# Differential attention in a written order of steps, and the last FFN tile's last accumulator in two passes of 256 columns

## The chip, the core and the metric

The kernel runs on one core of a Trainium2 chip. The core has five engines that each work through their own queue of instructions: PE (TensorE, matrix products into the accumulator memory PSUM), DVE (VectorE), ACT (ScalarE), POOL (GpSimd) and SP (SyncE, which here only issues DMA transfers). They meet through semaphores. Loading a matmul's stationary operand is shown as a row of its own (PEld). PSUM has eight banks of 128 × 512 float32.

The metric is device time in microseconds of one execution of the whole program. Lower is better.

## What is computed

A two-layer decoder trunk on 512 tokens with 1024 features. Layer 0 mixes latent attention and differential attention, layer 1 dilated and stick-breaking attention; each is followed by a gated ConvFFN. Every branch is normalised before and after.

```python
def diff_attention(q1, q2, k1, k2, v, lam, slopes):        # 4 heads, q and k 64 wide, v 128 wide
    ...
        def probs(qb, kf):
            s = jnp.einsum('bhqd,bhkd->bhqk', qb, kf).astype(jnp.float32) * scale + bias
            return jax.nn.softmax(jnp.where(causal, s, -jnp.inf), axis=-1)

        p = probs(a1, k1) - lam * probs(a2, k2)
        return jnp.einsum('bhqk,bhkd->bhqd', p.astype(v.dtype), v)
    ...
    o_diff = rms_norm(o_diff, subln_g) * (1.0 - lam_init)
    return jnp.concatenate([heads_last(o_mla), heads_last(o_diff)], axis=-1) @ w_out

def conv_ffn(h, w_up, conv_w, conv_b, w_down):
    u = causal_dwconv(h @ w_up, conv_w, conv_b)
    gate, up = jnp.split(u, 2, axis=-1)
    return (jax.nn.silu(gate) * up) @ w_down

def reference(x, ...):
    ...
        x = x + rms_norm(h, ev_post_g[j])                  # after each mixer
        h = conv_ffn(rms_norm(x, ffn_pre_g[i]), ffn_w_up[i], ffn_conv_w[i], ffn_conv_b[i], ffn_w_down[i])
        x = x + rms_norm(h, ffn_post_g[i])
    return x
```

## The kernel before

**Tiles.** The 512 tokens are four row tiles of 128, worked in the order 3, 2, 1, 0 (`ORDER`). Every large product is computed from two parts of each operand, a high part that ACT rounds (`wh`, `xh`) and a low part that DVE gets by subtracting the high part (`wl`, `xl`); `mm3` (L261) issues three matmuls for one product: high by high and the two mixed ones. The weights come through `Weights`: `load` (L47) issues the DMA on SP into one of three raw buffers, `split` (L71) makes the two parts, and `next` keeps `depth` weights made ahead.

**Who sets the order.** Outside of `manual_schedule` blocks a scheduler orders each engine's instructions by data and buffers; inside such a block the engines that it names run in the order of the program text. Banks of PSUM come from `bank(tag, ...)` (L107), by tags: three of tag a, two of s, one each of t, o, n. A matmul into a bank waits until the previous content has been read.

**Differential attention** is lines 832 to 922. For each of the four heads and each row tile i it has these steps, each a function: `score` (two score products with 64 rows each, into the two banks of tag s; then for each a DVE instruction that adds the distance table and finds the minimum, L611, and an exponential on ACT with its sum, L615; then on DVE reciprocals and the weighted difference of the two rows, L856 to L859), `turn` (transposes of the combined row on PE, L622, copied out of PSUM by ACT or DVE in turn, L625 and L627), `value` (the product with the values, L870, scaled by DVE, L872, squared and summed by ACT, L874, and three small steps of `rstd` on POOL), `norm` (L881), and after a head's last tile `finish` (four transposes, L888, and the split of the head's output). Tile i has i + 1 blocks of 128 keys, so the widest unit (i = 3) has 512 columns and the narrowest 128.

`skewed` (L267) emits these in program order, the units one step apart, and after every second step one filler: the projections of queries and keys of heads 1 to 3 (`diff_qk`, 24 wide matmuls each), then the first halves of the output projection of tiles 3 and 2 (`project`, 12 wide matmuls each). The scheduler then decides the order on the engines. One thing is forced:

```python
with tc.high_priority():
    for z in range(2):
        m = PE.matmul(s_ps[z][:, :w], dq[h][r, i * P:(i + 1) * P], dk[h][r, :w],
                      start=True, stop=True)
        if z:
            tc.keep_in_program_order(m)
        else:
            for n in reads:
                tc.add_manual_dep(m.ins, n, SYNC, reason="both banks")
```

The first of a pair of scores also waits until both banks have been read, so that the two go one behind the other.

After it comes the output projection of layer 0 (L927 to L949), already in a written order: for each tile the products, the normalisation of the tile before, and the transposes for the FFN.

**The end** is L520 to L535, the last FFN's tail. The FFN's down projection is computed with fewer products from sums and differences of weight blocks; of this only the last step matters here. Six accumulators a, b, c for s = 0 and 1 each get their last twelve matmuls by `bank_done` (L513). Accumulator a gives a tile's left half; the right half of tiles 3 and 1 is `uu` − b, the left half of tiles 2 and 0 is `uu` − c. The order is a, b, c for s = 0 (tiles 3 and 2), then a, b, c for s = 1 (tiles 1 and 0). `part_of` (L217) subtracts (L222), squares and sums on ACT (L230) and multiplies by the gain on DVE (L225); `rstd` (L174) adds and takes the power on POOL (L178 to L181); `store` (L256) scales and adds the residual in two halves on DVE (L258) and issues their DMAs, on SP but for the right half of the last tile, which ACT issues.

## Time and profile before

| | |
|---|---|
| median of the runs shown | 1158.38 us (1157.7 to 1159.26, 3 runs) |
| the profiled execution: its own time | 1158.78 us |
| its span in the trace | 1157.0 us |
| granted PE clock, mean | 0.997 |
| last instruction that issues a transfer | 1153.88 us, on ACT |

The profile shows one execution. Engines are PE, PEld, DVE, ACT, POOL and SP, and a name like L622 is a line of the program. A row of the timeline has start and duration in us, engine, line, operation, output and inputs with their shapes, how many instructions were merged (x), and in brackets the idle time of the engine before it and what ended it. A row of a group has busy time, mean ns of one instruction, and the idle time before them with what ended it. A row of the waits has who waited for whom, the total, the number of times and the longest. The end of a matmul is modelled: it is drawn until its result is out, while the next may start earlier, so distances from start to start tell the rate. A product of full float32 operands (scores, values) shows as two records.

### The profile page before, as it was taken

The page shows a single profiled execution, that of the slowest core. Times are in us where ns is not written, and L with a number is a line of the kernel's source. Part 1 is how long each engine was busy: PE and PEld are TensorE (multiplying, and loading weights), DVE is VectorE, ACT ScalarE, POOL GpSimd, SP SyncE. Part 2 cuts the span into 40 slices and gives each one's busy share as a digit, 9 for nine tenths or more (in the row PEclk, how much of TensorE's full clock was granted, in tenths as well). Part 3 has the DMA queues.
Part 4 walks back from the last instruction along what each step waited for, and adds up shares of the span by engine and source line. Part 5 has one row for each costly group of instructions (what it writes and reads, how often), then busy time and mean ns, then how long its engine had stood idle before and what let it go on. Part 6 is the DMA issues. An engine that isn't in the chain of part 4 may idle for free. (4 is left out here: it accounts for less than half of the span.)

```text
span 1157.0 us, 15177 instructions
## 1 busy us (share of the span) xinstructions
PE 1140.5 (99%) x5656; PEld 939.4 (81%) x5656; DVE 810.9 (70%) x1424; ACT 557.2 (48%) x942; POOL 58.4 (5%) x138
## 2 busy tenths in 40 slices
PE   8999999999999999999999999999999999999997
PEld 7876667898888888888888877898988888888885
DVE  6677676367666667898974565577676666689895
ACT  5565555245443443456643554545533433435662
POOL 2100021110000000000030000003000000000001
PEclk9999999999999999999999999999999999999999
DMA  7310521034223233355736213222233323225461
GB/s 282 119 64 1 166 78 37 37 131 128 91 92 107 93 91 89 103 154 159 243 97 189 83 55 95 90 74 110 77 111 107 92 91 108 93 82 147 145 200 73
DMA packets 39049, 126.81 MB, mean 110 GB/s; under 512 B 4672, under 2 KB 6336, under 8 KB 38848
## 3 DMA queue, kind: packets, MB, share of 16 engines
q1 hardware_dynamic: 37056, 122.11, 33.4%
q10 hardware_dynamic: 1920, 3.74, 1.1%
q8 instruction: 44, 0.72, 0.3%
q14 instruction: 29, 0.24, 0.1%
HBM read 117.95 MB, written 6.29 MB: 107 GB/s over the span
## 5 line engine op out<-in xcount | busy, mean ns | idle before, releaser
L73 DVE TENSOR_TENSOR wl<-wraw,wh 128x1024 fp32r<-128x1024 f32 (+1 forms) x202 | 244.4, 1218 | 174.3 <-ACT wh L72 174.0
L72 ACT CAST wh<-wraw 128x1024 fp32r<-128x1024 f32 (+1 forms) x202 | 209.4, 1046 | 280.8 <-PE u L264 179.5
L263 PE MATMUL u<-xh,wh 128*128 128x512 f32 (+1 forms) x768 | 285.4, 372 | 0.0
L264 PE MATMUL u<-xl,wh 128*128 128x512 f32 (+1 forms) x768 | 285.3, 371 | 0.0
L265 PE MATMUL u<-xh,wl 128*128 128x512 f32 (+1 forms) x768 | 285.2, 371 | 0.0
L263 PEld LDWEIGHTS u<-xh,wh 128*128 128x128 f32 x768 | 144.7, 188 | 25.0
L265 PEld LDWEIGHTS u<-xh,wl 128*128 128x128 f32 x768 | 144.7, 188 | 24.9
L264 PEld LDWEIGHTS u<-xl,wh 128*128 128x128 f32 x768 | 144.7, 188 | 24.9
L264 PE MATMUL acc<-wl,gh 128*128 128x512 f32 x248 | 96.5, 389 | 0.0
L265 PE MATMUL acc<-wh,gl 128*128 128x512 f32 x248 | 96.5, 389 | 0.0
L263 PE MATMUL acc<-wh,gh 128*128 128x512 f32 x248 | 96.4, 390 | 0.0
L417 ACT ACTIVATE y<-y 128x512 f32<-128x512 f32 x44 | 27.7, 632 | 85.0 <-DVE y L415 84.9
L412 ACT ACTIVATE y<-u,cw 128x512 f32<-128x512 f32 x88 | 67.5, 775 | 1.7 <-PE u L265 1.7
L415 DVE SCALAR_TENSOR_TENSOR y<-u,cw,y 128x510 f32<-128x510 f32 x88 | 65.6, 747 | 2.5
L413 DVE SCALAR_TENSOR_TENSOR y<-u,cw,y 128x511 f32<-128x511 f32 x88 | 65.1, 744 | 0.9 <-ACT y L412 0.9
L178 POOL TENSOR_TENSOR rv<-ms,epst 128x1 f32<-128x1 f32 x40 | 11.5, 287 | 908.3 <-ACT junk L230 837.9
L263 PEld LDWEIGHTS acc<-wh,gh 128*128 128x128 f32 x248 | 46.6, 188 | 10.2 <-issue 0.5
L265 PEld LDWEIGHTS acc<-wh,gl 128*128 128x128 f32 x248 | 46.6, 188 | 9.6
L264 PEld LDWEIGHTS acc<-wl,gh 128*128 128x128 f32 x248 | 46.6, 188 | 9.6
L263 PE MATMUL apt<-xh,wh 128*128 128x512 f32 x128 | 50.6, 396 | 0.0
L264 PE MATMUL apt<-xl,wh 128*128 128x512 f32 x128 | 50.0, 391 | 0.0
L265 PE MATMUL apt<-xh,wl 128*128 128x512 f32 x128 | 49.9, 390 | 0.0
(298 smaller groups left out, 1903.4 us busy)
## 6 DMA issues: line engine op xcount, KB each, us to landing
wraw<-in_ffn_w_up SPq DMA_DIRECT2D x88, 512.0 KB, 3.6
wraw<-in_ffn_w_down SPq DMA_DIRECT2D x44, 512.0 KB, 3.7
wraw<-in_od_w_dqk SPq DMA_DIRECT2D x12, 512.0 KB, 3.8
wraw<-in_ffn_w_down SPq DMA_DIRECT2D x22, 256.0 KB, 2.6
wraw<-in_ev_w_dqk SPq DMA_DIRECT2D x8, 512.0 KB, 4.0
wraw<-in_ev_w_out SPq DMA_DIRECT2D x8, 512.0 KB, 3.6
spill<-X SPq DMA_DIRECT2D x8, 512.0 KB, 2.6
X<-spill SPq DMA_DIRECT2D x8, 512.0 KB, 6.6
```

Source lines behind the costliest of these rows:

```text
L72: self.nc.scalar.copy(h[:, :w], raw[:, :w])
L73: self.nc.vector.tensor_tensor(l[:, :w], raw[:, :w], h[:, :w].bitcast(F32), ALU.subtract)
L178: POOL.tensor_tensor(v[:, :n], ms, epst[:, :n], ALU.add)
L263: PE.matmul(o, lh, rh, start=first, stop=False, skip_group_check=more)
L264: PE.matmul(o, lh, rl, start=False, stop=False, skip_group_check=more)
L265: PE.matmul(o, ll, rh, start=False, stop=last, skip_group_check=more)
L412: ACT.activation(y[:, z], u, AF.Identity, bias=c[:, 3:4], scale=c[:, 2:3])
L413: DVE.scalar_tensor_tensor(y[:, z, 1:], u[:, :S - 1], c[:, 1:2], y[:, z, 1:], ALU.mult, ALU.add)
L415: DVE.scalar_tensor_tensor(y[:, z, 2:], u[:, :S - 2], c[:, 0:1], y[:, z, 2:], ALU.mult, ALU.add)
L417: ACT.activation(y[:, 0], y[:, 0], AF.Silu)
```

## The change

The differential attention gets an order written out by hand for PE, DVE, ACT and POOL, and some of its steps change engine or form. The last FFN's tail gets a new order of accumulators, its last one is split into two halves of 256 columns, and the second half is accumulated from zero in another bank (its earlier content is subtracted beforehand).

The steps of the attention, cut:

```diff
+                def score(h, i):
...
+                    ps = [bank("s", "sps")[:, :w] for _ in range(2)]
+                    for z in range(2):
+                        r = slice(z * 64, (z + 1) * 64)
+                        PE.matmul(ps[z], dq[h][r, i * P:(i + 1) * P], dk[h][r, :w], start=True, stop=True)
+                    st = sc.tile([P, 8], F32, tag="st", name="st", bufs=11)
...
+                def exps(a):
+                    e, st = a
+                    for z in range(2):
+                        ACT.activation(e[z], e[z], AF.Exp, bias=st[:, 1 - z:2 - z], scale=-1.0,
+                                       accum_out=st[:, 3 - z:4 - z])
+
+                def combine(a):
+                    e, st = a
+                    DVE.reciprocal(st[:, 4:6], st[:, 2:4])
+                    DVE.scalar_tensor_tensor(st[:, 6:7], st[:, 4:5], st[:, 3:4], neglam[:], ALU.mult, ALU.mult)
+                    DVE.scalar_tensor_tensor(e[0], e[1], st[:, 6:7], e[0], ALU.mult, ALU.add)
+                    return e[0], st
 
                 def turn(h, i):
-                    return lambda s: transposed(sc, s, i + 1, i % 2, "t")
+                    return lambda a: (transposed(sc, a[0], i + 1, True, "t"), a[1])
...
-                        DVE.tensor_scalar(otok[:, i], o[:], v[:, 2], None, ALU.mult)
+                        ACT.activation(otok[:, i], o[:], AF.Copy, scale=st[:, 5:6])
+
                         jk = sc.tile([P, P], BF16, tag="jk", name="jk")
-                        ACT.activation(jk[:], otok[:, i], AF.Square, scale=P ** -0.5, accum_out=v[:, 3])
-                        return rstd(v[:, 3])
+                        ACT.activation(jk[:], otok[:, i], AF.Square, accum_out=st[:, 7:8])
+                        r = chp.tile([P, 1], F32, tag="rr", name="rr", bufs=4)
+                        POOL.tensor_tensor(st[:, 7:8], st[:, 7:8], epsp[:], ALU.add)
+                        POOL.tensor_tensor(r[:], st[:, 7:8], mhalf[:, 0:1], ALU.pow)
+                        return r
```

All transposed tiles are now copied by ACT, two reciprocals become one of two columns, and the factor of the mean goes into the gain (`subg`) and the constant (`epsp`). The projections become generators, `qk_parts` with eight steps and `parts_of` with four, each step three wide matmuls (one `mm3`); tile 1's first half joins the fillers. The order:

```diff
-                wout = [W2.next() for _ in range(2)]
+                wout = []
...
+                early = [(i, half) for i in (3, 2, 1) for half in range(2)]
+                fills = [qk_parts(h, z) for h in range(1, 4) for z in range(2)]
+                fills += [parts_of(i, half, 0) for i, half in early]
...
+                plan = ((6, 2),) + ((2, 2),) * 11 + ((2, 1),) * 4 + ((1, 0), (1, 1), (1, 2), (0, 2))
+                depth, W.depth = W.depth, 0
+                with tc.manual_schedule(engines={PE.engine, DVE.engine, ACT.engine, POOL.engine}):
+                    for n in range(len(units) + 4):
+                        if n < len(units):
+                            a = score(*units[n])
+                        if n in (3, 6, 9):
+                            wout.append(W2.next())
+                        elif len(wout) < 4:
+                            W.ahead(min(len(W.made) + 1, W.pos - len(busy) + 5))
+                        elif n == 15:
+                            W.ahead(W.pos + 4)
+                        if n < len(units):
+                            exps(a)
+                        fill(plan[n][0])
+                        if n >= 1 and n - 1 < len(units):
+                            turned_[n - 1] = turn(*units[n - 1])(scored.pop(n - 1))
+                        if n >= 2 and n - 2 < len(units):
+                            valued[n - 2] = value(*units[n - 2])(turned_.pop(n - 2))
+                        fill(plan[n][1])
+                        if n >= 3 and n - 3 < len(units):
+                            norm(*units[n - 3])(valued.pop(n - 3))
+                        if n < len(units):
+                            scored[n] = combine(a)
+                        if n >= 7 and n % 4 == 3:
+                            finish(n // 4 - 1)(None)
+                    fill(1000)
```

So in round n PE runs the scores of unit n, some fill steps, the transposes of unit n − 1, the values of unit n − 2 and more fill steps; weights are made one in a round instead of `depth` ahead.

The tail, cut to the second half of it (before this come, in the same manner, a, b and c for s = 0, then c for s = 1, and each tile is stored one accumulator later):

```diff
+                        DVE.tensor_tensor(t1[:, q4], uu[:, 1, 256:], bk["b", 1][:, 256:], sub)
...
+                        a = bank_done("a", 1)
+                        times(t1, lo, a)
+                        square(m1, 0, a)
+                        store(0, t0, r0, out)
+                        v = chp.tile([P, 4], F32, tag="rv", name="rv", bufs=4)
+                        POOL.tensor_tensor(v[:, 0:1], m1[:, 0:1], epst[:, 0:1], add)
+                        b = bank_done("b", 1, slice(0, 256))
+                        DVE.tensor_tensor(uu[:, 1, :256], uu[:, 1, :256], b[:, :256], sub)
+                        square(m1, 1, uu[:, 1, :256])
+                        times(t1, q3, uu[:, 1, :256])
+                        POOL.tensor_tensor(v[:, 1:2], v[:, 0:1], m1[:, 1:2], add)
+                        bk["b", 1] = bank("n", "acc")
+                        b = bank_done("b", 1, slice(256, S), True)
+                        DVE.tensor_tensor(t1[:, q4], t1[:, q4], b[:, 256:], sub)
+                        DVE.tensor_tensor_reduce(out=tmp[:, :256], in0=t1[:, q4], in1=t1[:, q4], scale=1.0 / D,
+                                                 scalar=v[:, 1:2], op0=mul, op1=add, accum_out=v[:, 2:3])
+                        r = chp.tile([P, 4], F32, tag="rr", name="rr", bufs=4)
+                        POOL.tensor_tensor(r[:, 0:1], v[:, 2:3], mhalf[:, 0:1], ALU.pow)
+                        times(t1, q4, t1[:, q4])
+                        store(1, t1, r, out)
```

`times` multiplies by the gain on DVE, `square` squares and sums on ACT. The last tile is now tile 1, and its right half's DMA is the one that ACT issues.

165 lines of the change are left out of this document (95 added, 70 removed).

## The prediction

> **What bounds the kernel now.** I read the page first, then busy time by stretch, the waits of the tensor engine alone, its timeline around each wait, the groups of the differential stage and the last microseconds.
>
> ```profile
> PE 1140.5 (99%) x5656; PEld 939.4 (81%) x5656; DVE 810.9 (70%) x1424; ACT 557.2 (48%) x942; POOL 58.4 (5%) x138
> ```
>
> ```profile
> core 0 of [0], span 1157.0 us
> core 0: us, PE busy (x) PEld busy (x) DVE busy (x) ACT busy (x) POOL busy (x), PEclk, DMA share, GB/s
> 127.00:206.00 79.00, 75.13 (x390) 54.14 (x389) 58.15 (x186) 44.17 (x124) 13.36 (x31) 1.00 0.29 87
> 206.00:246.00 40.00, 40.00 (x202) 33.82 (x202) 19.80 (x26) 14.25 (x31) 7.72 (x19) 1.00 0.17 61
> 254.00:262.00 8.00, 8.00 (x69) 8.00 (x68) 1.90 (x3) 1.17 (x2) 0.00 (x0) 1.00 0.02 7
> ```
>
> PE is busy for 99% of the span, so only what shortens PE's own sequence, or the work before its first and after its last matmul, can move the end. In 127–206, the differential stage, PE is idle for 79.00 − 75.13 = 3.87 us at full clock; the projection after it has no idle time. The waits of PE there, with total, times and longest:
>
> ```profile
> PE tpp L622 <- DVE s L858: 1.5, 1, 1.5
> PE sps L845 <- DVE st L611: 1.2, 2, 0.8
> ```
>
> These two are late DVE results: a combined softmax, and score banks not yet read. The other place where PE does not decide is the end:
>
> ```profile
> 1145.19 0.39 PE L263 MATMUL acc<-wh,gh 128*128 128x512 f32 x1
> ...
> 1148.37 0.39 PE L265 MATMUL acc<-gh,gl 128*128 128x512 f32 x1
> ```
>
> From the first of these rows to the last are 14 steps, (1148.37 − 1145.19)/14 = 0.227 us each. The last matmul ends at 1148.37 + 0.39 = 1148.76, and 8.2 us of span follow.
>
> **The change part by part.**
>
> *Stage: the waits that go.* The idle time understates a wait, since a matmul's drawn end reaches past the next possible start. From start to start:
>
> ```profile
> 136.15 0.39 PE L265 MATMUL aqk<-xh,wl 128*128 128x512 f32 x1
> 138.03 0.63 PE L622 MATMUL tpp<-ident,s 128*128 128x128 f32 x4 [1.50 <-DVE s L858]
> ```
>
> ```profile
> 173.32 0.39 PE L263 MATMUL aqk<-xh,wh 128*128 128x512 f32 x1
> 173.55 0.39 PE L264 MATMUL aqk<-xl,wh 128*128 128x512 f32 x1
> 173.86 0.70 PE L845 MATMUL sps<-dqk 64*128 64x256 f32 x4
> ```
>
> A projection matmul takes 0.23 us to the next (173.32 to 173.55), and 0.31 where a score follows without a wait (173.55 to 173.86). 136.15 to 138.03 is then 1.57 too long, 0.07 more than the idle time shown; short waits hide up to 0.2. With 0.1 on each of seven waits the 3.87 become about 4.6 us. In the new order the producers get more room. For the widest unit (four key blocks), from score to combined row:
>
> ```profile
> L611 DVE CUSTOM_DVE_ANT_0 s<-sps,alibi 128x512 f32<-128x512 f32 x8 | 5.2, 683 | 0.0
> L611 DVE DVE_READ_ACCUMULATOR2_ANT st<- 128x1 f32 x32 | 2.6, 82 | 0.0
> L615 ACT ACTIVATE s<-s,st 128x512 f32<-128x512 f32 x8 | 5.7, 716 | 0.8 <-DVE st L611 0.7
> L615 ACT ACTIVATION_READ_ACCUMULATOR s<-s,st 128x1 f32 x32 | 6.0, 187 | 0.0
> L856 DVE RECIPROCAL den<-st 128x1 f32<-128x1 f32 x16 | 2.6, 160 | 0.9 <-ACT s L615 0.6
> L857 DVE SCALAR_TENSOR_TENSOR den<-den,st,neglam 128x1 f32<-128x1 f32 x16 | 3.4, 215 | 1.5 <-ACT s L615 1.3
> L858 DVE SCALAR_TENSOR_TENSOR s<-s,den 128x512 f32<-128x512 f32 x4 | 3.0, 750 | 0.0
> ```
>
> That is 2 × (0.68 + 0.08) + 0.72 + 0.19 + 0.16 + 0.22 + 0.75 = 3.6 us. Between this score and its transposes the written order puts six fill steps of three matmuls (18 × 0.227 = 4.1) and the next score, about 5 us with nothing else counted (five steps in the last head, 4.2). A weight's low part in the same unit lengthens the chain, as does the copy of a finished key projection, which now stands in DVE's queue ahead of the combining:
>
> ```profile
> L73 DVE TENSOR_TENSOR wl<-wraw,wh 128x1024 fp32r<-128x1024 f32 x12 | 14.6, 1221 | 3.5 <-ACT wh L72 3.5
> L649 DVE COPY dqk<-aqk 128x512 f32<-128x512 f32 x3 | 2.1, 689 | 2.4 <-PE aqk L265 2.4
> L872 DVE TENSOR_SCALAR otok<-o,den 128x128 f32<-128x128 f32 x16 | 5.5, 342 | 2.0 <-PE o L870 2.0
> ```
>
> With the 1.22 the widest chain is 4.8 us, still under 5; the last head's widest unit has no weight. Behind the key copy wait the two small DVE operations and a 256-wide combining (between 0.35 and 0.75, say 0.5): 0.69 + 0.16 + 0.22 + 0.5 = 1.6 us from the last fill, against a narrow score (0.4) and one fill pair (1.36): 0.2 to spare, three times. Handing over between engines can eat that, so I take 0.3 us of new waits, from 0 to 1.5 (one more like the longest that goes).
>
> *Who becomes busier.* DVE gives up 16 scalings (16 × 0.342 = 5.5), 16 of 32 reciprocals (16 × 0.16 = 2.6) and eight copies of transposed tiles (at most 8 × 0.69, by the copy row above, 5.5): 58.15 falls to 45 to 48 us. ACT takes the scalings and copies, at DVE's prices for want of an ACT row: 44.17 rises to 55 at most. Both lie well under PE's 75 and cost nothing by load; if the cover is lost, it is a late row for PE, already in the 0 to 1.5. The squares lose their scale and the variance constant is multiplied instead: no time. POOL's three small steps a unit stand a whole unit ahead of the normalising that needs them.
>
> *The first pair of scores.* Before, it was split over the preceding attention; a pair issued together runs at the same time:
>
> ```profile
> 114.77 1.12 PE L845 MATMUL sps<-dqk 64*128 64x512 f32 x2
> ```
>
> ```profile
> 129.35 0.39 PE L263 MATMUL aqk<-xh,wh 128*128 128x512 f32 x1
> ```
>
> ```profile
> 147.85 1.13 PE L845 MATMUL sps<-dqk 64*128 64x512 f32 x4
> ```
>
> The row at 114.77 is one of two halves, drawn 1.12 long (x2); a whole pair (x4) is drawn 1.13. Some 1.05 is saved, once both halves lose what the drawing adds, unless their places were waits anyway; value projections take these places, so I count 0.9 of 0 to 1.05. The pair now follows the value projection, whose end was at 129.35, where the key projection begins, and comes to lie near 127.4 without the halves; and its exponentials stand behind a weight cast whose raw buffer comes free late: the subtraction that frees it follows these products in DVE's queue, and then a load takes 4.0 us to land.
>
> ```profile
> 125.50 0.23 DVE L808 CUSTOM_DVE_ANT_0 lj<-lamb 128x64 f32<-128x64 f32 x1 [1.61 <-DMA lamb<-in_ev_lam]
> ```
>
> ```profile
> wraw<-in_ev_w_dqk SPq DMA_DIRECT2D x8, 512.0 KB, 4.0
> ```
>
> So 125.5 + 0.3 + 1.2 + 4.0 gives a landing near 131; a cast (about as long as its subtraction, 1.2), two exponentials 1.8, the two small operations and the combining 1.1: ready near 135.1. Its transposes come after the pair (1.1), eight fill steps, a score (0.8) and two more steps, 30 × 0.227 = 6.8: near 136.1. Hidden, with 1 us of cover. SP's queue keeps its loads; two of the output weights move behind the last two query/key weights, and 13 us or more lie between a later raw buffer's release and its cast.
>
> *More changes of kind on PE.* Between the value projection and the next FFN, the written order enters small matmuls from wide ones 34 times, the old one 26 times. Each entry costs 0.31 − 0.23 = 0.09: 8 × 0.09 = 0.7 us lost; 0 if the last small one overlaps as much, 1.5 if the way back costs it too.
>
> *The projection's cover.* Row tile 1's first half (24 wide matmuls, 5.5 us) moves into the stage, so half of that cover leaves the wait for tile 3's transposes. They come 12 × 0.227 = 2.7 us after tile 2's last matmul; the product (0.69) and two normalisings (0.75 each, the row of that form) that must run first take 2.2. Nothing is lost, and up to 0.5 if it were.
>
> *The end.* What follows the last matmul now:
>
> ```profile
> 1149.18 0.68 DVE L222 TENSOR_TENSOR t<-uu,acc 128x512 f32<-128x512 f32 x1
> 1149.39 0.55 POOL L181 TENSOR_TENSOR rr<-rv,mhalf 128x1 f32<-128x1 f32 x1
> ...
> 1149.96 0.63 ACT L230 ACTIVATE junk<-t 128x512 bf16<-128x512 f32 x1 [1.41 <-DVE t L222]
> ...
> 1150.82 0.61 POOL L180 TENSOR_TENSOR rv<-rv,ms 128x1 f32<-128x1 f32 x1 [0.72 <-DVE t L258]
> 1151.31 0.68 DVE L225 TENSOR_TENSOR t<-t,gain 128x512 f32<-128x512 f32 x1
> 1151.51 0.88 POOL L181 TENSOR_TENSOR rr<-rv,mhalf 128x1 f32<-128x1 f32 x1
> 1152.43 1.42 DVE L258 SCALAR_TENSOR_TENSOR t<-t,rr,X 128x512 f32<-128x512 f32 x2 [0.44 <-POOL rr L181]
> ```
>
> Subtract, square, add, power, scale: 1148.76 to 1152.43 + 1.42 = 1153.85, 5.1 us. In the new tail the last pass ends at the same place: 24 matmuls of 256 columns at 8.00/69 = 0.116 take 2.78 against 12 × 0.227 = 2.72. After it come a 256-wide subtraction (0.35 to 0.4), the fused square and sum, the power and two scalings. The fused step needs the first half's sum. That half's accumulator ends near 1147.4, but DVE is still at tile 0: its accumulator ends near 1148.76 − 2.78 − 2.72 = 1143.3, subtraction, square, read and POOL (0.68 + 0.63 + 0.19 + 0.2 + 0.61 + 0.55) give its factor near 1146.3, tile 1's first product holds DVE to 1146.7, tile 0's scalings (1.42) to 1148.2. Then subtraction 0.4, square 0.4, its read 0.19, POOL 0.61 and some handing over give 1149.9. Fused step 0.5 (256-wide, between half and whole of 0.68 + 0.08), power 0.55 to 0.88, scalings 1.42: 1152.4 to 1152.7 against 1153.85. I take 1.2 us gained, from 0.6 (POOL slower) to 1.9 (tile 0 stored earlier). The output's way to memory is the same.
>
> The power took 0.88 while a DVE product with two SBUF operands ran from 1151.31, 0.55 at 1149.39 beside a subtraction from PSUM. The Trainium skill (SBUF — State Buffer, SBUF: two separate sides) says that GpSimd and such a DVE operation exclude each other for a whole instruction; the trace agrees with 0.88 against 0.55. By it the new product beside the power costs its 0.35, by the quiet row nothing. Halving the columns doubles the weight loads; in 254–262, 69 matmuls of 256 columns and 68 loads fit into 8.00 us. The Trainium skill (TensorE: Matmul & The Clock Gate, Part 3: Packing small matmuls) lets a weight load overlap a running matmul only for other row groups; with the page's 128/1.2 = 107 ns for a load, 12 more would cost 1.3 us, an estimate, and take the tail's gain away. The trace disagrees.
>
> *Sum.* 4.6 + 0.9 − 0.7 − 0.3 + 1.2 = 5.7 us. The profiled execution took 1158.78 us (span and 1.8 around it), giving 1153.1; the median shown is 0.4 lower, 1158.38, giving 1152.7.
>
> **The rivals.** *Waits come back.* One queue per engine is now in a fixed order, so one late item delays everything behind it. If the slim places (0.2 us behind key copies, under 1 us in wide units with a weight) each miss by 0.2 to 0.3, some 12 units lose 3.2 us: 1155.9. For it speaks that the longest waits now are for DVE, whose order gets no looser; against it that every producer gets a fill step or two more distance.
>
> *Slower: PE waits in every unit.* PE itself is now in written order, so a late row stops the fills behind it, which the scheduler could still pull forward. It decides once the chain runs 1.8 us beyond my 3.6 in every unit: from 0.4 us past the cover of 5, 16 × 0.4 = 6.4 exceed the 1.2 + 0.9 + 4.6 − 0.7 = 6.0 gained. At 0.6 us it is 9.6 against 6.0: 1162. Loads of 48 and 55 us at most against 75 speak against it; 1.5 us lost before to a single late row shows that it can be.
>
> *The stage gives nothing.* The idle 3.87 us are only moved to its start and its last head; the tail alone stays: 1157.2. Against it: the last value has 18 wide matmuls (4.1 us) before its transposes, and square, POOL and normalising need some 2.5.
>
> *The narrow passes show their weight loads.* The 68 loads keep their path busy for the whole 8.00 us, 0.118 each; were 12 of them unhidden in the tail, 12 × 0.118 = 1.4: 1154.1. Against it: 69 matmuls fitted beside them.
>
> **How the numbers follow.** Forecast 0.68, waits back 0.17, stage nothing 0.06, narrow loads 0.02, slower 0.07. About 0.2% (2.3 us) is what a measurement can tell from no change, so below 1156.1 is faster: 0.68, 0.02 and most of the second case, 0.82; the same 0.11; slower 0.07. All terms at their best ends give 4.7 + 1.05 + 1.9 = 7.6, 1150.7; the range goes from 1151.0 to 1156.4, which takes in the second case and leaves out some 0.17.
>
> **What would show it.** Right: PE idle in the stage under 1 us; the first score pair as one group of four; the last tile's final DMA issue 1.2 us nearer to the last matmul. Wrong: PE waiting for a combined row in many units, casts on ACT waiting for DMA in front of exponentials, PE's 256-wide matmuls at over 0.15 us each, or the fused step waiting past 1150.3. Matmuls elsewhere should keep their order and spacing.

## The result, and the profile after

| | before | after |
|---|---|---|
| median of 6 runs, us | 1158.15 (1157.58 to 1159.26) | 1151.05 (1150.84 to 1151.89) |
| profiled execution, us | 1158.78, span 1157.0 | 1151.33, span 1149.5 |

The ratio of the times is 0.9938, 95% interval 0.9925 to 0.9951. The gain is 7.1 us by the medians and 7.5 us by the two profiled executions; 5.7 was forecast. The kernel before was run again beside each group of experiments below, with medians of 1157.3 to 1158.1, so the medians put the gain at 6.3 to 7.1. The profiled execution of before, 1158.78, lies high among its runs.

Where the time went is read most sharply inside the traces. First the stage: the first matmul of a query/key projection, long before the stage, and the first matmul of the FFN behind it, from PE's timeline of the kernel before (columns: start us, us, engine, line, operation, tiles, shape):

```profile
36.09 0.40 PE L263 MATMUL aqk<-xh,wh 128*128 128x512 f32 x1
...
242.33 0.28 PE L263 MATMUL u<-xh,wh 128*128 128x256 f32 x1
```

The same two places after, and between them the first pair of scores, which stands right behind the value projection:

```profile
36.02 0.39 PE L263 MATMUL aqk<-xh,wh 128*128 128x512 f32 x1
...
127.07 1.13 PE L889 MATMUL sps<-dqk 64*128 64x512 f32 x4
128.13 0.50 PE L263 MATMUL aqk<-xh,wh 128*128 128x512 f32 x1
...
236.54 0.28 PE L263 MATMUL u<-xh,wh 128*128 128x256 f32 x1
```

From the first to the last, 206.24 us became 200.52: 5.7 us. This distance is called the *stage distance* from here on; starting at a fixed matmul, it leaves out how soon the program begins. The value projection ended 129.35 − 36.09 = 93.26 after the first row; now it ends 127.07 − 36.02 = 91.05 after it, 2.21 earlier, and the pair that now follows takes 128.13 − 127.07 = 1.06: 1.15 net. The remaining 4.57 lie behind it. Busy time by stretch after (columns as in the prediction: stretch, length, then PE, PEld, DVE, ACT and POOL, clock, DMA share, GB/s):

```profile
127.00:206.00 79.00, 79.00 (x410) 57.30 (x410) 49.57 (x147) 50.30 (x146) 13.26 (x32) 1.00 0.27 86
206.00:246.00 40.00, 40.00 (x224) 34.47 (x223) 25.02 (x32) 18.13 (x36) 7.95 (x21) 1.00 0.29 104
```

PE's 3.87 us without work are gone, DVE's load went from 58.15 to 49.57, ACT's from 44.17 to 50.30, and PE's waits have no row left. (The same 79 us now hold 410 matmul records instead of 390.)

From the first FFN matmul to the end of the last matmul nothing changed: 906.43 us before, 906.45 after. The second gain comes behind that, in the tail:

```profile
1142.71 0.28 PE L265 MATMUL acc<-wh,gl 128*128 128x256 f32 x1
1142.72 0.42 ACT L529 ACTIVATE junk<-uu 128x256 bf16<-128x256 f32 x1 [1.07 <-DVE uu L567]
1143.02 0.42 DVE L573 TENSOR_TENSOR t<-t,acc 128x256 f32<-128x256 f32 x1
1143.05 0.18 ACT L529 ACTIVATION_READ_ACCUMULATOR junk<-uu 128x1 f32 x1
1143.37 0.19 POOL L570 TENSOR_TENSOR rv<-rv,ms 128x1 f32<-128x1 f32 x1 [1.03 <-ACT junk L529]
1143.60 0.48 DVE L574 CUSTOM_DVE_ANT_0 tmp<-t,rv 128x256 f32<-128x256 f32 x1 [0.15 <-POOL rv L570]
1144.01 0.08 DVE L574 DVE_READ_ACCUMULATOR2_ANT rv<- 128x1 f32 x1
1144.12 0.42 DVE L532 TENSOR_TENSOR t<-t,gain 128x256 f32<-128x256 f32 x1
1144.17 0.79 POOL L577 TENSOR_TENSOR rr<-rv,mhalf 128x1 f32<-128x1 f32 x1 [0.61 <-DVE rv L574]
1144.99 1.41 DVE L258 SCALAR_TENSOR_TENSOR t<-t,rr,X 128x512 f32<-128x512 f32 x2 [0.44 <-POOL rr L577]
...
1146.44 0.35 ACTq L259 DMA_DIRECT2D out_dram<-t  x1
```

The last matmul ends at 1142.71 + 0.28 = 1142.99 and the last scaling at 1144.99 + 1.41 = 1146.40, 3.41 later, where it was 5.09 (1148.76 to 1153.85). That is 1.68. Stage 5.72, tail 1.68, the same middle, and 0.07 at the start make the 7.5 of the spans.

### The profile page after: what moved, and what is told of

It reads as the page before. It is cut to its first block, busy times and chain, and to the rows that moved or that the text cites. A ratio compares the mean times of both kernels' runs of the same rounds, so it can differ in the third digit from the quotient of the medians.

```text
span 1149.5 us, 15154 instructions
## 1 busy us (share of the span) xinstructions
PE 1138.7 (99%) x5668; PEld 939.3 (82%) x5668; DVE 805.6 (70%) x1389; ACT 565.1 (49%) x966; POOL 58.0 (5%) x139
## 4 chain that ended last, share of the span: by engine, by line
PE 96%; issue 1%; POOL 1%; DMA 1%; DVE 1%; ACT 0%; SPq 0%; POOLq 0%; DVEq 0%; ACTq 0%
PE u L264 14%; PE u L263 14%; PE u L265 14%; PE acc L263 6%; PE acc L264 6%; PE acc L265 6%; PE apt L263 3%; PE apt L264 3%; PE apt L265 3%; PE ao L263 2%; PE ao L265 2%; PE ao L264 2%; PE sps L773 2%; PE aqk L263 1%; PE av L263 1%; PE aqk L265 1%
## 5 line engine op out<-in xcount | busy, mean ns | idle before, releaser
L264 PE MATMUL acc<-wl,gh 128*128 128x512 f32 (+1 forms) x250 | 96.9, 388 | 0.0
L265 PE MATMUL acc<-wh,gl 128*128 128x512 f32 (+1 forms) x250 | 96.9, 388 | 0.0
L263 PE MATMUL acc<-wh,gh 128*128 128x512 f32 (+1 forms) x250 | 96.8, 388 | 0.0
```

Of the source, the lines that this page charges most:

```text
L263: PE.matmul(o, lh, rh, start=first, stop=False, skip_group_check=more)
L264: PE.matmul(o, lh, rl, start=False, stop=False, skip_group_check=more)
L265: PE.matmul(o, ll, rh, start=False, stop=last, skip_group_check=more)
```

## The experiments

Each run is the changed kernel with one edit, unless said otherwise. The columns of this table are worked out as above from each run's trace; the times are medians (one run each for the two marked 1), those of before the medians beside the same group of runs.

| run | time | before | stage distance | last matmul to scalings' begin | to their end |
|---|---|---|---|---|---|
| before | 1158.15 | | 206.24 | 3.67 | 5.09 |
| after | 1151.05 | 1158.15 | 200.52 | 2.00 | 3.41 |
| e1 stage alone | 1152.51 | 1157.56 | 200.53 | 3.68 | 5.09 |
| e2 tail alone | 1156.31 | 1157.56 | 205.33 | 2.00 | 3.42 |
| e3 one pass | 1151.84 | 1157.56 | 200.52 | 2.80 | 4.21 |
| e4 gain in PSUM | 1150.52 | 1157.56 | 200.50 | 1.76 | 3.17 |
| e5 384 and 128 | 1150.78 (1) | 1157.32 | 200.52 | 1.60 | 3.01 |
| e6 blocked add | 1151.95 (1) | 1157.32 | 200.48 | 2.27 | 3.68 |
| e7 more visits | 1151.51 | 1157.47 | 200.89 | 2.02 | 3.43 |
| e8 fewer visits | 1150.61 | 1157.47 | 200.27 | 2.01 | 3.42 |
| e9 back on DVE | 1151.25 | 1157.47 | 200.44 | 2.01 | 3.42 |
| e10 turn first | 1154.69 | 1157.47 | 204.46 | 2.01 | 3.42 |
| e11 scheduler | 1151.54 | 1157.32 | 200.48 | 2.01 | 3.42 |
| e12 both gains | 1150.57 | 1158.14 | 200.34 | 1.76 | 3.18 |
| e13 scheduler and DVE | 1156.57 | 1158.14 | 205.59 | 2.01 | 3.42 |
| e15 lumps | 1158.83 | 1158.14 | 207.87 | 2.01 | 3.42 |

Six runs of after still span 1 us, while the stage distance of five runs with an untouched stage (e1, e3 to e6) lies within 0.05 us. So differences under half a microsecond are read in the last three columns, not in the times.

**The two parts by themselves.** e1 has the changed stage and the old final block, with the old place of the ACT store; e2 has the old stage and the changed final block with what it calls.

> The changed stage with the old tail. If the two parts act apart, this gains over the kernel before what its trace and the changed kernel's show for the stage: first FFN matmul at 236.54 instead of 242.33, so 5.8 us, near 1152.4. By the prediction's terms the stage gives 4.5, near 1153.7. A rival, that the parts meet (earlier loads of the stage change what is late in the tail), gives neither: under 4 or over 7. In the trace PE should have no wait between 127 and 206, and the time from the last matmul to the end of the last scaling should be the 5.09 us of before.

> The old stage with the changed tail. From the traces: the scalings end 3.41 us after the last matmul instead of 5.09, and the span 6.51 instead of 8.24 after it: 1.7 us gained over the kernel before, near 1156.4. The prediction's term is 1.2, near 1156.9. If the tail's gain needs the stage's earlier start, it is under 0.6. The small POOL addition ahead of the fused step should take 0.19 us, as in the changed kernel, and not the 0.61 that the prediction put down.

Measured: e1 gains 5.05 us by the medians (ratio 0.9956, 0.9943 to 0.9968), 5.7 by the stage distance, and has the old tail to the hundredth. e2 gains 1.25 by the medians (0.9990, 0.9981 to 0.9999; 0.1 to 2.2 us), 1.67 in the tail, and its POOL addition took the 0.19. The parts act apart.

e2's stage distance is 0.9 shorter than before's although nothing in that stage was edited, and all four compute engines run the same instructions in the same order there in both traces. What differs is when weights land. ACT's casts of weights in the kernel before, and the same two in e2:

```profile
131.98 1.05 ACT L72 CAST wh<-wraw 128x1024 fp32r<-128x1024 f32 x1 [1.55 <-DMA wraw<-in_ev_w_out]
...
134.91 1.05 ACT L72 CAST wh<-wraw 128x1024 fp32r<-128x1024 f32 x1 [1.17 <-DMA wraw<-in_ev_w_out]
```

```profile
130.99 1.04 ACT L72 CAST wh<-wraw 128x1024 fp32r<-128x1024 f32 x1 [1.06 <-DMA wraw<-in_ev_w_out]
...
133.23 1.05 ACT L72 CAST wh<-wraw 128x1024 fp32r<-128x1024 f32 x1 [0.47 <-DMA wraw<-in_ev_w_out]
```

Counted from the first key projection behind the value projection (129.35 before, 128.86 in e2), e2's casts begin 0.5 and 1.2 us sooner. The subtraction that makes the low part waits for the second cast, and the combined row for which PE waits longest (136.15 to 138.03) stands behind that subtraction in DVE's queue; in e2 it is ready 1.2 sooner, and 0.4 of that is lost again at a score. So 0.9 of the stage's 5.7 belongs to this one execution of the kernel before; why its weights landed later is not shown. The changed stage has no such spread in the five traces named above.

**One pass instead of two.**

```diff
-                        b = bank_done("b", 1, slice(0, 256))
...
+                        b = bank_done("b", 1)
+                        DVE.tensor_tensor(t1[:, hi], uu[:, 1], b, sub)
+                        DVE.tensor_tensor_reduce(out=tmp[:, hi], in0=t1[:, hi], in1=t1[:, hi], scale=1.0 / D,
+                                                 scalar=v[:, 0:1], op0=mul, op1=add, accum_out=v[:, 2:3])
...
+                        times(t1, hi, t1[:, hi])
```

> The changed kernel, but its last accumulator in one pass of 512 columns in one bank, with the same order of tiles and the fused square. If the order and the fused square carry the tail's gain and two passes only shorten the last operations: last matmul to end of scalings = subtraction 0.68 + fused 0.84 + power 0.88 (beside a 512-wide product) + scalings 1.41 and 0.2 to 0.3 of handing over = 4.0 to 4.1 instead of 3.41, so 0.6 to 0.7 us slower than the changed kernel, 1151.7. If the second pass carries the gain: 1.2 us or more slower, 1152.3 or above. If the passes cost PE what they save at the end: no difference.

The tail of e3, from the timeline:

```profile
1142.35 0.39 PE L265 MATMUL acc<-wh,gl 128*128 128x512 f32 x1
1142.78 0.69 DVE L566 TENSOR_TENSOR t<-uu,acc 128x512 f32<-128x512 f32 x1 [0.58 <-PE acc L265]
1143.61 0.75 DVE L567 CUSTOM_DVE_ANT_0 tmp<-t,rv 128x512 f32<-128x512 f32 x1
...
1144.40 0.69 DVE L532 TENSOR_TENSOR t<-t,gain 128x512 f32<-128x512 f32 x1
1144.45 1.05 POOL L570 TENSOR_TENSOR rr<-rv,mhalf 128x1 f32<-128x1 f32 x1 [2.20 <-DVE rv L567]
1145.54 1.41 DVE L258 SCALAR_TENSOR_TENSOR t<-t,rr,X 128x512 f32<-128x512 f32 x2 [0.44 <-POOL rr L570]
```

The scalings begin 1145.54 − 1142.74 = 2.80 after the last matmul: 3.67 before, 2.80 with the new order of tiles and the fused square, 2.00 with the second pass too. The tail's gain is made about half by each (0.87 and 0.80); the new order and the fused square were not taken apart. It is 0.8 slower than the changed kernel by the medians too; the expected 0.6 to 0.7 was too small by the power, which took 1.05 beside a product of 0.69.

**POOL beside DVE.** e4 puts the gain's last 256 columns into a PSUM bank early; e6 moves a product behind the last subtraction.

```diff
+                        gq = bank("t", "acc")
+                        ACT.copy(gq[:, :256], g_post[:, q4])
                         b = bank_done("b", 1, slice(0, 256))
...
-                        times(t1, q4, t1[:, q4])
+                        DVE.tensor_tensor(t1[:, q4], t1[:, q4], gq[:, :256], mul)
```

> The changed kernel, with the last 256 columns of the gain copied to a PSUM bank ahead of the second pass, so that the last DVE product, which runs beside the power on POOL, reads one operand from SBUF and one from PSUM. If POOL is kept back by a DVE operation with two SBUF operands, the power takes 0.55 instead of 0.79 and the scalings begin 0.25 us earlier: 0.25 us faster. If the power's 0.79 has another cause (any DVE work beside it, the handing over of the sum), it stays at 0.79 and the time too.

The tail of e4:

```profile
1141.71 0.28 PE L265 MATMUL acc<-wh,gl 128*128 128x256 f32 x1
...
1143.17 0.55 POOL L579 TENSOR_TENSOR rr<-rv,mhalf 128x1 f32<-128x1 f32 x1 [0.61 <-DVE rv L576]
1143.19 0.42 DVE L580 TENSOR_TENSOR t<-t,acc 128x256 f32<-128x256 f32 x1
1143.75 1.41 DVE L258 SCALAR_TENSOR_TENSOR t<-t,rr,X 128x512 f32<-128x512 f32 x2
```

The product still runs beside the power and still takes 0.42, but the power is back to 0.55; the scalings begin 1.76 after the last matmul instead of 2.00. So the operands' place made the 0.24, not the company of DVE work.

```diff
-                        times(t1, q3, uu[:, 1, :256])
...
                         DVE.tensor_tensor(t1[:, q4], t1[:, q4], b[:, 256:], sub)
+                        times(t1, q3, uu[:, 1, :256])
```

> The changed kernel with the product over the third quarter moved behind DVE's last subtraction, so that it runs beside the POOL addition ahead of the fused step. If that addition is kept back by a DVE operation with two SBUF operands, it takes 0.4 to 0.6 instead of 0.19, as the prediction priced it, and the fused step begins near 1144.0, 0.4 us later; the scalings end near 1146.8. If the addition only takes 0.19 because it is small, it ends at 1143.56 all the same, and the fused step waits for DVE alone, to 1143.9.

The tail of e6:

```profile
1142.96 0.28 PE L265 MATMUL acc<-wh,gl 128*128 128x256 f32 x1
...
1143.62 0.42 DVE L532 TENSOR_TENSOR t<-uu,gain 128x256 f32<-128x256 f32 x1
1143.63 0.45 POOL L569 TENSOR_TENSOR rv<-rv,ms 128x1 f32<-128x1 f32 x1 [1.03 <-ACT junk L529]
1144.12 0.48 DVE L574 CUSTOM_DVE_ANT_0 tmp<-t,rv 128x256 f32<-128x256 f32 x1
```

The same addition that took 0.19 takes 0.45 beside a product from two SBUF operands and ends with it (1144.08 and 1144.04). The Trainium skill (SBUF — State Buffer, SBUF: two separate sides) describes this as a lock that the one which starts first holds for a whole instruction; both runs agree. The fused step, 0.27 later than in the changed kernel (0.4 expected), was held here by DVE's own product as much as by the addition; the 0.27 is not the addition's alone.

**A narrower second pass** (all 256 become 384 in the first pass and 128 in the second).

> The changed kernel with the last accumulator in passes of 384 and 128 columns. For the rival that narrow passes show their weight loads: if a load of 0.19 us is hidden down to any width, a 128-wide matmul takes 0.06 and the second pass 0.7 us; if there is a floor, as 0.11 a piece for the 128-wide value matmuls shows, 12 x 0.11 = 1.3 us and the last matmul ends about 0.5 later than in the changed kernel. The end moves less, since the sum of the first pass is late: the wider subtraction and square push the fused step from 1143.60 to near 1143.95, its own work is shorter by 0.2: 0.1 us slower, from -0.2 to +0.4.

The second pass of e5, its second and its last matmul:

```profile
1141.45 0.27 PE L264 MATMUL acc<-gl,gh 128*128 128x128 f32 x1
...
1142.56 0.28 PE L265 MATMUL acc<-wh,gl 128*128 128x128 f32 x1
```

Ten steps lie between them, 0.111 each: as much as 256 columns (0.12). The floor is there, and 256 columns stand just above it. The scalings begin 0.40 sooner after the last matmul, but the two passes last 1142.84 − 1139.28 = 3.56 instead of 1142.99 − 1139.95 = 3.04: 0.12 lost in all, as expected.

**What a visit to small matmuls costs.** e7 puts one of the fill steps between transposes and values; e8 puts all fill steps of a unit ahead of the transposes, so that its values run straight into the next score.

```diff
+                            fill(plan[n][1] > 0)
                             valued[n - 2] = value(*units[n - 2])(turned_.pop(n - 2))
-                        fill(plan[n][1])
+                        fill(plan[n][1] - (n >= 2 and plan[n][1] > 0))
```

```diff
-                plan = ((6, 2),) + ((2, 2),) * 11 + ((2, 1),) * 4 + ((1, 0), (1, 1), (1, 2), (0, 2))
+                plan = ((6, 2),) + ((4, 0),) * 11 + ((3, 0),) * 4 + ((1, 0), (1, 1), (1, 2), (0, 2))
```

> The changed kernel with a fill step also between a unit's transposes and the values that follow: in ten units PE goes into small matmuls once more, 10 more visits in the stage with the same matmuls. By the prediction's price of an entry, 0.09 each, 0.9 us slower. By the start-to-start rows of the changed kernel a visit costs nothing net: the wide matmul after it is 0.10 longer, the last small one 0.08 shorter (0.03 instead of 0.11), the wide one before it 0.01 to 0.02 longer: 0.02 to 0.03 each, 0.3 us slower in all. Waits should not appear.

> The changed kernel with all of a unit's fill steps between its score and the transposes, so that the values run straight into the next score: 15 fewer visits to small matmuls, same matmuls. By the prediction's price, 0.09 each, 1.4 us faster. By the start-to-start rows: a small matmul ahead of a score takes 0.205, against 0.03 + 0.10 + 0.10 for leaving and entering a score anew, so 0.02 each: 0.3 us faster at most. The distance from a score to its own transposes stays six fill steps, so no waits should come.

Measured in the stage distance: e7 +0.37 for 10 more visits, e8 −0.25 for 15 fewer. Little of either is the visits. In e7 one wait is new, ahead of the last head's transposes: 206.31 to 206.90, 0.59 where 0.23 is usual, which is 0.35 of the 0.37. e8 lacks two short waits of the changed kernel (0.26 together, shown in the next section), and has a delay of about that size in the projection (208.51 to 209.23, two steps of usually 0.23). Its plan also puts eight fill steps between a score and its own transposes, not the six that its expectation names. What is left for a visit is at most 0.02, not 0.09. PE's timeline of the changed kernel around two visits:

```profile
142.55 0.40 PE L265 MATMUL aqk<-xh,wl 128*128 128x512 f32 x1
142.88 0.49 PE L889 MATMUL sps<-dqk 64*128 64x128 f32 x4
143.30 0.50 PE L263 MATMUL aqk<-xh,wh 128*128 128x512 f32 x1
143.64 0.39 PE L264 MATMUL aqk<-xl,wh 128*128 128x512 f32 x1
...
144.56 0.40 PE L265 MATMUL aqk<-xh,wl 128*128 128x512 f32 x1
144.80 0.38 PE L668 MATMUL tpp<-ident,s 128*128 128x128 f32 x2
```

The wide matmul ahead of a score takes 0.33 to the next start, but the one ahead of transposes 0.24, as between wide ones (0.23). The first wide one behind a score takes 0.34. e7 and e8 change visits between transposes and values, and between values and the next score. The visits that the change adds are of a third kind, between a score and the transposes behind it: behind the first pair a wide matmul follows a pair of scores 7 times before and 15 times after. These e10 takes away, below.

**What removed the waits.** Three runs undo one thing each, two more undo two: e9 puts the scaling of the values and every second copy of transposes on DVE again; e10 moves a unit's fill steps behind its values; e11 takes the stage out of the written order (without the tie that, before, held the two products of a pair of scores together); e13 is e9 and e11 together; e15 is e11 with the fills in whole products of eight steps ahead of every second unit.

```diff
-                    return lambda a: (transposed(sc, a[0], i + 1, True, "t"), a[1])
+                    return lambda a: (transposed(sc, a[0], i + 1, i % 2, "t"), a[1])
...
-                        ACT.activation(otok[:, i], o[:], AF.Copy, scale=st[:, 5:6])
+                        DVE.tensor_scalar(otok[:, i], o[:], st[:, 5:6], None, ALU.mult)
```

> The changed kernel with the scaling of the values and every second copy of transposed tiles back on DVE, as before, in the new written order: 16 x 0.34 and eight copies go from ACT to DVE, whose load in the stage rises from 49.6 to about 59 us of 79. If the order and the distance from score to transposes removed the waits, PE waits at most 0.5 us, in the units where a key copy leaves 0.15 to 0.28 us of slack. If the lighter DVE removed them, most of the 3.6 us come back: 1154 or more.

```diff
-                plan = ((6, 2),) + ((2, 2),) * 11 + ((2, 1),) * 4 + ((1, 0), (1, 1), (1, 2), (0, 2))
+                plan = ((6, 2),) + ((0, 4),) * 11 + ((0, 3),) * 4 + ((1, 0), (1, 1), (1, 2), (0, 2))
```

> The changed kernel with all of a unit's fill steps behind its values, so that from a score to its own transposes there are four fill steps instead of six, 2 x 0.68 = 1.36 us less. By the slack that the changed kernel's trace shows (transposes begin 0.15 to 0.28 us after the combined row in units 2, 6 and 10, 1.4 to 3.5 us in the others) PE waits 1.1 to 1.2 us in three units and none in the others: 3.4 us slower, the waits named at the transposes for a combined row. If the written order as such removed the waits, wherever the fills stand, it stays within 0.5 us of the changed kernel. 15 fewer visits to small matmuls would give 0.3 back.

```diff
-                with tc.manual_schedule(engines={PE.engine, DVE.engine, ACT.engine, POOL.engine}):
+                if True:
                     for n in range(len(units) + 4):
```

> The changed kernel's steps of the stage, but the engines' order in it left to the scheduler: PE's order stays nearly the same (the last head's fills move), DVE's and ACT's order of casts, combining, scaling and copies changes. If the written order on DVE and ACT is what removes the waits, most of the 3.6 us come back, 1154.5. If the form of the steps does it (more fill steps between producer and user, less on DVE), it stays within 0.7 us of the changed kernel.

Measured: e9 and e11 lose nothing (200.44 and 200.48), though e9's DVE is back at 56.88 us:

```profile
127.00:206.00 79.00, 79.00 (x410) 57.33 (x409) 56.88 (x171) 42.51 (x122) 14.08 (x32) 1.00 0.25 86
```

e10 loses 3.9 us (3.4 expected), with these waits of PE (total, times, longest) in the window from 127 to 246:

```profile
PE tpp L668 <- DVE s L907: 4.4, 3, 1.6
PE tpp L668 <- DVE odl L172: 0.7, 2, 0.3
```

Three waits for a combined row are the three units that the expectation named. The second row it had not: the transposes behind a finished head now come before the split of that head's output has cleared their bank. The waits are 5.1 us and the stage lost only 3.9: fifteen visits between a score and its transposes are gone too, which gives some back, by the rows above about 0.1 each (0.34 instead of 0.23). So the distance between a score and its transposes is needed; the order on DVE and ACT, or DVE's load, looked as if neither mattered.

> New steps and their spread of fills, but DVE has the scalings and half the copies as before, and the engines' order is left to the scheduler. Each alone cost nothing (200.44 and 200.48 us from the first key projection to the first FFN matmul, 200.52 in the changed kernel). If the spread of the fills is what removed the waits, it stays within 0.5 us of 200.5. If the lighter DVE and the written order can stand in for one another, so that only without both the waits come back, it rises by 2 us or more towards the 206.24 of before, of which 1.1 is the start.

e13 loses 5.1 us, 205.59, 3.1 of it in named waits of PE. Each alone costs nothing, both together nearly all. DVE's timeline of e13:

```profile
166.03 1.21 DVE L73 TENSOR_TENSOR wo<-wraw,wo 128x1024 fp32r<-128x1024 f32 x1
167.15 0.35 DVE L919 TENSOR_SCALAR otok<-o,st 128x128 f32<-128x128 f32 x1
...
168.93 0.35 DVE L932 SCALAR_TENSOR_TENSOR otok<-otok,rr,subg 128x128 f32<-128x128 f32 x1 [0.91 <-POOL rr L925]
169.19 0.69 DVE L172 TENSOR_TENSOR odl<-tpo,odh 128x512 fp32r<-128x512 f32 x1
```

and what PE does then:

```profile
169.94 0.33 PE L668 MATMUL tpp<-ident,s 128*128 128x128 f32 x1 [0.71 <-DVE odl L172]
```

The scheduler put a weight's low part (1.21) ahead of the small scaling L919. Scaling, square, power and normalising follow one another late, the split L172 stands behind the normalising in DVE's queue, and PE's next transposes need the bank that the split reads. In e9 the written order has the scaling ahead of such work; in e11 the scaling is on ACT. Either one breaks this chain. Some 0.8 of e13's loss is something else: in three of its sixteen pairs of scores the two products no longer run together as they do in e11, and the pair takes longer (195.20 to 196.21, 1.01, where such a pair takes 0.63 in the changed kernel, 192.42 to 193.05).

```diff
-                plan = ((6, 2),) + ((2, 2),) * 11 + ((2, 1),) * 4 + ((1, 0), (1, 1), (1, 2), (0, 2))
+                plan = ((0, 0),) * 20
...
-                with tc.manual_schedule(engines={PE.engine, DVE.engine, ACT.engine, POOL.engine}):
+                if True:
                     for n in range(len(units) + 4):
+                        if n % 2:
+                            fill(8)
```

> New steps and the lighter DVE, but the fills issued as before: a whole product of eight fill steps ahead of every second unit, and the order left to the scheduler, which pulls some of them apart again. If the spread of the fills removed the waits, PE waits come back about as in the kernel before: 3 to 5 us in the stage for combined rows and unread score banks, near 204 to 206 us from the first key projection to the first FFN matmul. If the new steps (exponentials and combining apart, work on ACT) removed them, it stays within 0.7 us of 200.5.

e15 loses 7.4 us, 207.87, more than all that the stage gained, with the lighter DVE and the new steps in place. Named waits are only 2.7 us of it. Another 2.5 come from the scores: four of the sixteen pairs are torn apart, all 256 wide. One of them, from PE's timeline of e15:

```profile
134.60 0.70 PE L889 MATMUL sps<-dqk 64*128 64x256 f32 x2
135.22 0.50 PE L263 MATMUL aqk<-xh,wh 128*128 128x512 f32 x1
...
136.45 0.70 PE L889 MATMUL sps<-dqk 64*128 64x256 f32 x2
```

Each half takes as long by itself (0.62) as the whole pair does together (0.63). The tie that prevents this in the kernel before is not in the new `score`, where the written order makes it needless, and e15 does not put it back. The remaining 2.1 are not separated. So the fill steps' distance is needed (e10), and besides it either the written order or the lighter DVE (e9, e11, e13). What the spread of the fills is worth by itself e15 does not show.

**Both small gains** (e8's plan and e4's bank).

> The changed kernel with the fill steps of the fewer-visits run and the gain in PSUM of the tail run together. The two touch different places: 0.25 us from the stage (first key projection to first FFN matmul 200.27 instead of 200.52) and 0.24 from the tail (last matmul to scalings 1.76 instead of 2.00), so 0.5 us faster than the changed kernel, near 1150.5. If the earlier start of the tail or the moved fills cost something elsewhere: no difference.

The tail's 0.24 is there in full (1.76), the stage's 0.25 in part (200.34). By the medians it is 0.5 faster than the changed kernel, 0.9929 (0.9915 to 0.9942) of before against 0.9938 (0.9925 to 0.9951); the intervals overlap, and its profiled execution has the same span, 1149.4, with 0.4 us more in the untouched middle.

## Why the prediction came out as it did

The direction, both places and both mechanisms were right. Two terms of the sum were too small, the waits in the stage and the end, and one came out near its value for another reason. Measured against forecast, place by place:

- *Waits that go*, 4.6: this is the step that failed in the stage. The forecast took the idle time, 3.87, and 0.1 for each of seven waits. Added up from start to start behind the first pair, against the usual steps (0.32 into a score, 0.23 into other small matmuls), the kernel before loses 4.6 ahead of small matmuls, 0.4 between transposes and the values behind them (148.91 to 149.46), and 0.7 in seven steps between value matmuls, 0.21 each, where all of the changed kernel take 0.11: 5.8. What delays these seven is not shown. After the longest wait, at 136.15, which is 1.65 (the text took off the step into a score, where transposes follow), the longest is this one, 1.20 where 0.32 is usual:

```profile
169.49 0.40 PE L264 MATMUL aqk<-xl,wh 128*128 128x512 f32 x1
170.69 0.92 PE L845 MATMUL sps<-dqk 64*128 64x384 f32 x4 [0.81 <-DVE st L611]
```

  e2's trace of the same stage gives 4.9 when added up like this, so 0.9 of the 5.8 is the late weights of one execution.
- *New waits*, 0.3: they are there, and where the text put them. It left 0.2 to spare behind each key copy, and the trace shows two such units wait a little. PE's timeline of the changed kernel at one of them:

```profile
162.74 0.40 PE L265 MATMUL aqk<-xh,wl 128*128 128x512 f32 x1
163.11 0.41 PE L668 MATMUL tpp<-ident,s 128*128 128x128 f32 x2
```

  From 162.74 to 163.11 are 0.37 where 0.24 is usual; the same 0.37 stands between 181.53 and 181.90. That is 0.13 twice, 0.26 against 0.3. The view of waits lists neither, because a matmul's drawn end covers them.
- *More changes of kind*, −0.7: about −0.8, for another reason, so the size is luck. The text carried the 0.31 ahead of a score over to every entry, but of the added entries most go into transposes, where the step is 0.24. What costs is the way back from scores: eight more wide matmuls stand right behind a pair and take 0.34 instead of 0.23. The text had the way back only in its bound of 1.5. 5.8 − 0.3 − 0.8 makes 4.7, and 4.57 were measured.
- *First pair*, 0.9 of at most 1.05: 1.15. The value projection ended 2.21 earlier, 0.1 more than the two halves took from start to start (113.00 to 114.06 and 114.77 to 115.82). Whether the rest is the cost of entering twice was not tried by itself.
- *The end*, 1.2: 1.68. This is the other term that was mis-sized, by this step: "POOL 0.61" for the addition ahead of the fused step. The 0.61 quoted for it (1150.82) had been taken beside a scaling from two SBUF operands. In the new order nothing of that kind runs there, and it took 0.19, so the fused step began 0.61 after the last matmul where the text has 1.14. e6 puts such a product back, and it takes 0.45. The prediction had noticed the same effect on the power, 0.88 against 0.55, and did not carry it over. The upper end, 1.9, named another cause (tile 0 stored earlier).
- *Narrow passes*: no unhidden loads at 256 columns, 0.12 each where the text has 0.116; e5 shows where that ends.
- *Who becomes busier*: DVE 49.57 against 45 to 48, ACT 50.30 against 55 at most; neither costs by load. Why load did not matter was right only with the written order, as e13 shows.
- *Rivals*: waits in every unit, or many small ones, did not come; e10 shows that the point from which they would was near. It has two fill steps less room, and PE waits in three units.

The signs named: PE's idle time in the stage is 0, one cast on ACT waits for its DMA ahead of the first exponentials (1.25 us, at 129.12) and PE does not wait for it, the first pair is one group of four at 127.07, and the last DMA issue follows the last matmul by 1146.44 − 1142.99 = 3.45, against 1153.88 − 1148.76 = 5.12 before, 1.67 nearer.

Together: 1.2 of waits, 0.25 for the pair and 0.5 at the end were left out of 5.7; the other two terms came out as counted, and 0.2 is not placed. That makes the 7.4 that the two places gained between the two profiled executions, 0.9 of it by the late weights of the one before. The result, 1151.05, lies at the lower edge of the range.

Open: why runs of the kernel before spread over 2 to 3 us and those of the changed kernel over 1. The weights that land sooner or later, above, are one source; how much of the spread they make, the traces can't tell.

## What to carry to other kernels

Price a small operation by a row in which its neighbours are the ones it will have, not by the row of the same line: here 0.61 was the price of company. Where a producer and a user sit in written order, count the fill steps between them against the chain, with what stands in the queue; in e10 two steps less, 1.4 us, came back as waits of 1.3 to 1.6 us in the three units that had next to no slack. Undo safeguards in pairs as well as singly: two that can stand in for each other each look useless alone. And ask of each undoing what else it takes away: without the tie of the score pairs, e15 lost 2.5 us that have nothing to do with its question.

## What the runs showed of the hardware

- POOL's one-column operations that meet a DVE operation with two SBUF operands end shortly after it, by a time of their own: the power 0.42 after it in the changed kernel (1144.96 against 1144.54), 0.41 in e3 (1145.50 against 1145.09); the addition 0.04 after it in e6. Undisturbed they take 0.55 and 0.19. With the same 0.42 us of DVE work reading one operand from PSUM, the power is undisturbed.
- A 128-wide matmul with a fresh weight takes 0.111 from start to start, a 256-wide one 0.12, a 512-wide one 0.227: halving 512 columns is nearly free, halving 256 is not. The Trainium skill (TensorE: Matmul & The Clock Gate, LDWEIGHTS (loading the stationary operand)) gives a weight load by its columns over 1.2, which makes 107 ns for 128, an estimate; the 0.111 stands close to it. With wider matmuls the load is hidden, although all of them use the same rows.
- Going back and forth between wide and small matmuls costs by the place: a wide one takes 0.24 to a transpose but 0.33 to a score, and the first wide one takes 0.34 behind a score (0.23 between wide ones). Behind transposes or values it takes 0.31 too, but there the last small one takes only 0.03 instead of 0.11, so visits between transposes, values and the next score cost at most 0.02.
- Two score products of 64 rows, issued together, take as long as one: 0.63 for a 256-wide pair, 0.62 for one half by itself.
